# Second input phase: one of the seven block products as seven smaller ones, its operand sums stored and loaded, T3 formed later

## The chip, the cores and the metric

One NeuronCore of a Trainium2 chip runs the kernel. The metric is the time of one execution on the device, in microseconds (us); 911.04 us is the median of three executions of the kernel before (910.7 to 911.11). A profile records one further execution. The engines are TensorE (PE in the profile; PEld is its weight load), VectorE (DVE), ScalarE (ACT), GpSimd (POOL) and SyncE (SP), which only issues transfers.

## What is computed

One layer over 4096 frames of 1024 float32 channels (`DEPTH` is 1, so only the pooling mixer runs):

```python
def pool_mixer(h, in_w, group_w, group_b, scale, out_w):
    b, s, _ = h.shape
    u, gate = jnp.split(h @ in_w, 2, axis=-1)
    ug = u.reshape(b, s, POOL_GROUPS, POOL_GROUP_DIM)
    pooled = jnp.stack([trailing_mean(ug[:, :, g], w) for g, w in enumerate(POOL_WINDOWS)],
                       axis=2) - ug
    mixed = jnp.einsum('bsgc,gcd->bsgd', pooled, group_w) + group_b
    y = mixed.reshape(b, s, POOL_WIDTH) * scale * jax.nn.silu(gate)
    return y @ out_w

h = x + pool_mixer(rms_norm(x, norm_w), ...)
out = rms_norm(h, final_norm_w)
```

The windows are 2, 4, 8 and 16 frames. The large products are `h @ in_w` (1024 by 2048) and `y @ out_w` (1024 by 1024). The kernel has folded `group_w` into the first half of `in_w`.

## The kernel before

**Products.** Every product of a 1024-deep block is done by the Strassen-Winograd scheme: four quarters a11 to a22 of the data and four of the weights b11 to b22, and seven products P1 to P7 of sums of quarters instead of eight. On the data side the sums are S1 to S4, on the weight side T1 to T4. P3 is S4 x b22: S4 = a12 - S2, and b22 unchanged. Each float32 operand is split into a high half (ScalarE's copy, L165 in `split`, L167) and a low half (VectorE's subtraction, L159), both in TensorE's float32r type; a product takes three passes, high x high, high x low, low x high (`mm3`, L598). One product of a block of 1024 frames is 48 matmuls of 128 by 128 by 512 columns.

**Order of the work.** `steps` is one list: phase "a" (channels for windows 2 and 4 with their gate) for four blocks of 1024 frames, phase "b" (windows 8 and 16), which is the second input phase, for four blocks, and phase "o" (the output product) for eight blocks of 512 frames. Each block runs its seven products in the order P1, P2, P7, P6, P5, P4, P3 (`ORDER_IN`) or P1, P7, P6, P2, P5, P4, P3 (`ORDER_OUT`). The main loop (L1325) takes one step per turn: it issues loads up to three steps ahead (`load_reach`), splits the operands of the next step (`advance("split", ...)`), forms sums of the step after that (`form`), issues a pooling that is due (`pool_due`), then the matmuls and the evictions of this step (`run`). A scheduler then puts each engine's instructions in one fixed order, by the order of the program and by what it reckons to be ready; `tc.issue_after` sets an instruction behind another. What comes earlier in the program goes first where both are ready.

**Buffers.** Four operand tiles `op` go round, two for each step, so the split for the next step runs while TensorE works on this one. Eleven tiles `st` and eight tiles `vt` hold everything else (`Slots`); a load waits until its tile is free. Eight PSUM banks: P1, P2, P7, P4 in banks 0 to 3, P6, P5, P3 in banks 4 to 7. After P1 ScalarE copies its banks to banks 4 to 7, where P6, P5 and P3 are added on top.

**Sums of the data.** In phase a `form_in` (L547) forms the sums on VectorE and `split_halves` (L509) stores the operands of P1, P2, P7 and P4 to DRAM (`sd`) through the POOL queue. In phase b these four are loaded (`load_saved`, L528) and the other three, for P6, P5 and P3 (`form_s4`, L592), are formed again by VectorE: six operations on 128 x 1024 per block.

**Eviction and pooling.** P1's chain ends with P3, whose four banks ScalarE copies out (the last branch of `evict_in`, L806). After P5 and P4 VectorE adds the banks onto the rows, and ScalarE applies Silu to the gate. `pool` (L745) then forms the trailing means on VectorE. `pool_later` (L1116) says when: the half from P4 one step after it (two in the last block), the half from P3 two steps after it (five in the last).

**Weights.** Weights of phase b are formed during the last block of phase a (`load_wb`, `form_wb`, `split_wb`). T3, which two of them need, is formed from four stored tiles by `save_t3` (L289) at block 2, P7 of phase a. During block 3 of phase b the weights of the output product are loaded and split behind each step (`load_w`, L343); their sums were formed by `make_wo` (L335) in blocks 1 and 2, at P5.

**The seven inner products of phase o.** From the third block of phase o on, P2 of that phase is itself done by the scheme: `form_inner` (L643), `split_inner` (L669), `product_inner` (L689, matmuls at L701 of 256 columns). Block 1 sets four `st` tiles aside for its weight sums (`kept`).

```python
stages = (P6, P5, P4)
...
    advance("load", n, load, load_reach)
...
    advance("split", n, split_step, split_reach)
...
    pool_due(n)
...
    run(n)
```

Of the kernel before, what the change touches and what calls it, by code (L numbers as in the profile page):

```python
# [15 lines left out]
P = 128  # L16
D = 1024
# [18 lines left out]
class Slots:  # L36
# [4 lines left out]
    def __init__(self, tiles):  # L41
        self.free = deque((0, t) for t in tiles)
        self.used = {}

# [9 lines left out]
    def keep(self):  # L54

        return self.renew(self.free.popleft()[1])

# [7 lines left out]
def kernel(  # L65
# [54 lines left out]

    def renew(t):
        i = next(i for i, u in enumerate(sts) if u is t)
        return mem.tile([P, D], F32R, tag=f"st{i}", name=f"inner{i}")

    st.renew = renew
# [41 lines left out]
    def split(dst, src):  # L167
# [17 lines left out]
        for i in range(P1, P7 + 1)  # L185
# [4 lines left out]
            for i in (P1, P2, P7, P4)  # L190
# [97 lines left out]

    def save_t3():  # L289

        for h in range(2):
            us = []
            for k in (h, 2 + h):
                us.append(take())
                nc.sync.dma_start(out=us[-1], in_=wvd[k])
            with tc.issue_after(evicted[0]):
                sub(us[0], us[1], us[0])
            nc.sync.dma_start(out=t3d[h], in_=us[0])
            for u in us:
                give(u)  # L300
# [22 lines left out]
    def split_wb(i):  # L323
        for h in range(2):
            (u,) = parts.pop((i, h)).values()
            if i == P1:
                split_scaled(w[i][h], u, pair(norm_c, h, 0))
            elif i == P2:
                split_scaled(w[i][h], u, pair(norm_c, h, 1))
            else:  # L330
                split(w[i][h], u)
            if i != P6:
                give(u)
# [202 lines left out]
    def load_in(q, b, i):  # L536
        s = xs[b]
        if i == P1:
            s["11"] = load_saved(b, P1) if q else load_x(b, 0, 0)
        elif i == P2:  # L540
            s["12"] = load_saved(b, P2) if q else load_x(b, 0, 1)
        elif i == P7:
            s["21"] = load_saved(b, P7) if q else load_x(b, 1, 0)
        elif i == P6:
            s["22"] = load_saved(b, P4) if q else load_x(b, 1, 1)

    def form_in(q, b, i):  # L547

        s = xs[b]
        if i in (P1, P2):  # L550
            if q == 0:
                for u in s["11" if i == P1 else "12"]:
                    normalize(b, 0, u)
        elif i == P7:
            if q == 0:
                for h in range(2):
                    normalize(b, 1, s["21"][h])
                    sub(s["21"][h], s["11"][h], s["21"][h])
        elif i == P6:
            s["2"] = [take(pool=early if (q, b) == (0, 0) else None) for _ in range(2)]  # L560
            for h in range(2):
                if q == 0:
                    normalize(b, 1, s["22"][h])
                sub(s["2"][h], s["22"][h], s["21"][h])
            for u in s.pop("21"):
                give(u)
            if q == 0:
                give(rstd.pop(b))
        elif i == P5:
            for h in range(2):  # L570
                add(s["11"][h], s["2"][h], s["11"][h])
            if (q, b) != (0, 0):
                for u in s.pop("2"):
                    give(u)

    def split_in(q, b, i):
        s = xs[b]
        key = {P1: "11", P2: "12", P6: "2", P7: "21", P5: "11", P4: "22", P3: "12"}[i]
        later = q == 0 and b == 0 and i in (P1, P2)
        t = split_halves(s[key], None if q or later else sd[b].get(i))  # L580
        if later:
            stores.extend(zip(sd[0][i], s[key]))
        if i == P6 and (q or b):
            form_s4(b)
        if i not in (P1, P2, P7, P6):
            for u in s.pop(key):
                give(u)
        return t
# [19 lines left out]

    def product_in(i, t, sets, by_bank, between=None, behind=None):
        ps = sets[bank_of[i]]  # L610
# [194 lines left out]

    def evict_in(b, q, i, sets, seeds=4):  # L806
# [22 lines left out]
        elif i == P4:  # L829
            for c, u in enumerate(cells(ev["21"])):  # L830
                add(halved(u), plain(ps[c]), halved(u))
            for u in ev["21"]:
                copy(u, u, AF.Silu)
# [250 lines left out]
    def form(n):  # L1084
        kind, b, i = step(n)
        if kind in ("a", "b"):
            form_in(kind == "b", b, i)
# [16 lines left out]
    def run(n, between=None, behind=None, seeds=4):  # L1104
# [5 lines left out]
        else:  # L1110
            product_in(i, split_up.pop(n), sets, i == P1, between, behind)
            evict_in(b, 0 if kind == "a" else 1, i, sets, seeds)
# [3 lines left out]
    def pool_later(n):  # L1116
        kind, b, i = steps[n]
        if i == P4:
            args = (b, 0 if kind == "a" else 1, 1, ev.pop("22"), ev.pop("21"))
            wait = int(b == 0) if kind == "a" else 1 if b < NB - 1 else 2  # L1120
# [183 lines left out]
    def load_reach(kind, b, i):  # L1304
        return 4 if kind == "o" else 3
# [16 lines left out]
    stages = (P6, P5, P4)  # L1322
    stages = (P6, P5, P4)

    for n in range(2, len(steps)):  # L1325
# [17 lines left out]
        if kind == "o" and b == 1 and len(kept) < 4 and not inner_w:  # L1343
            while len(kept) < 4 and len(st.free) > 2:
                kept.append(st.keep())
            if len(kept) == 4:
                load_inner()
        elif kept:
            keep[0] = 0
        advance("split", n, split_step, split_reach)  # L1350
# [19 lines left out]
        pool_due(n)  # L1370
# [3 lines left out]
        run(n)  # L1374
        if kind == "a" and b == 2 and i == P7:
            save_t3()
# [5 lines left out]
        if kind in ("a", "b"):  # L1382
# [5 lines left out]
            if kind == "b" and b in (1, 2) and i == P5:  # L1388
                make_wo(b - 1)
# [58 lines left out]
```

## Time and profile before

| | |
|---|---|
| median of three executions | 911.04 us (910.7 to 911.11) |
| the profiled execution | 911.84 us |
| its span, first to last instruction | 909.7 us |
| mean granted TensorE clock | 0.997 |
| phase b, from about | 325 to 615 us |
| one block of phase b | 72.6 us |

The profile's page gives busy times per engine, slices of the span, the chain of work that ended last, and groups of equal instructions: line, engine, operation, output <- input, shapes, count, then busy time, mean ns of one, and idle time ahead of them with what ended it. In the timeline a row is start, duration, engine, line, operation, tiles, count, and in brackets the idle time before it. In a table by windows each engine has its busy time and, in brackets, its instructions. A wait row is engine, tile and line, what was waited for, total us, times, longest.

### The profile page before, as it was taken

What the parts mean: (1) busy time and instruction counts of PE and PEld (TensorE: products, weight loads), DVE (VectorE), ACT (ScalarE), POOL (GpSimd) and SP (SyncE); (2) the same over time, 40 slices, a digit from 0 to 9 for tenths busy, and PEclk for the clock granted to TensorE, in tenths of its full rate; (3) what the DMA queues carried; (4) which work ended last, traced back from release to release, by engine and by line L of the source; (5) the groups of instructions that cost most, each with busy time, mean ns of one, the idle gap of its engine ahead of it and who ended that gap; (6) DMA issues with size and microseconds to landing.
All of it is one profiled execution on the core that took longest, in us unless ns stands there. A gap on an engine that the chain in (4) does not pass through costs nothing.

```text
span 909.7 us, 11455 instructions
## 1 busy us (share of the span) xinstructions
PE 900.6 (99%) x4320; PEld 790.1 (87%) x4320; DVE 764.5 (84%) x909; ACT 461.8 (51%) x693; POOL 49.9 (5%) x124
## 2 busy tenths in 40 slices
PE   9999999999999999999999999999999999999997
PEld 7888888888888888888888888888888898888886
DVE  3889995985995997696798699699989878978886
ACT  7869547547446565355445545644424424335334
POOL 0020100100110000000000000000201001001000
PEclk9999999999999999999999999999999999999998
DMA  9977766577675454116616714636385464464332
GB/s 341 401 291 240 276 235 230 189 270 253 217 272 196 156 202 145 47 64 212 255 47 234 275 70 158 235 105 219 137 280 181 149 226 155 146 232 139 116 139 93
DMA packets 66807, 178.08 MB, mean 196 GB/s; under 512 B 6080, under 2 KB 23872, under 8 KB 66752
## 3 DMA queue, kind: packets, MB, share of 16 engines
q1 hardware_dynamic: 60176, 155.83, 48.8%
q0 software_dynamic: 5856, 20.46, 6.1%
q10 hardware_dynamic: 720, 1.06, 0.3%
q8 instruction: 34, 0.56, 0.2%
q14 instruction: 21, 0.17, 0.1%
HBM read 116.50 MB, written 60.83 MB: 195 GB/s over the span
## 4 chain that ended last, share of the span: by engine, by line
PE 91%; DMA 4%; DVE 3%; issue 1%; ACT 0%; SPq 0%; POOL 0%; DVEq 0%; ACTq 0%; POOLq 0%
PE bank L603 88%; PE bank L701 3%; DMA early<-in_wut 2%; DMA st<-in_x 1%; DMA vt<-yd 1%; DVE vt L1033 1%; PE bank L406 1%; DVE op L159 1%; DVE st L159 0%; DVE vt L916 0%; ACT st L943 0%; DVE vt L162 0%; DVE vt L711 0%; SPq L370 0%; DVE st L1033 0%
## 5 line engine op out<-in xcount | busy, mean ns | idle before, releaser
L603 PE MATMUL bank<-op,w 128*128 128x512 f32 x2688 | 580.9, 379 | 0.0
L603 PEld LDWEIGHTS bank<-op,w 128*128 128x128 f32 x2688 | 508.5, 189 | 71.8 <-ACT bank L165 0.4
L603 PE MATMUL bank<-w,op 128*128 128x512 f32 (+1 forms) x1212 | 262.2, 377 | 0.0
L603 PEld LDWEIGHTS bank<-w,op 128*128 128x128 f32 x1212 | 226.3, 189 | 30.7
L165 ACT ACTIVATE op<-st 128x1024 fp32r<-128x1024 f32 x129 | 134.7, 1053 | 142.2 <-PE bank L603 90.5
L159 DVE TENSOR_TENSOR op<-st,op 128x1024 fp32r<-128x1024 f32 x129 | 156.8, 1222 | 51.7 <-ACT op L165 51.3
L156 DVE TENSOR_TENSOR vt<-vt 128x1024 f32<-128x1024 f32 (+6 forms) x72 | 88.2, 1236 | 0.6
L159 DVE TENSOR_TENSOR op<-vt,op 128x1024 fp32r<-128x1024 f32 x43 | 52.5, 1222 | 19.8 <-ACT op L165 19.6
L165 ACT ACTIVATE vt<-bank 128x512 f32<-128x512 f32 x82 | 47.6, 593 | 41.4 <-PE bank L603 40.5
L165 ACT ACTIVATE op<-vt 128x1024 fp32r<-128x1024 f32 x43 | 45.1, 1053 | 39.3 <-PE bank L603 30.2
L159 DVE TENSOR_TENSOR st<-st,st 128x1024 f32<-128x1024 f32 (+1 forms) x43 | 47.0, 1111 | 2.3 <-ACT st L912 1.3
L165 ACT ACTIVATE bank<-bank 128x512 f32<-128x512 f32 x48 | 27.9, 581 | 32.9 <-PE bank L603 32.9
L1033 DVE TENSOR_TENSOR vt<-bank,vt 128x512 f32<-128x512 f32 (+1 forms) x55 | 37.1, 677 | 7.4 <-PE bank L603 7.0
L165 ACT ACTIVATE st<-bank 128x512 f32<-128x512 f32 x48 | 27.8, 593 | 28.7 <-PE bank L603 22.3
L207 POOL TENSOR_SCALAR oms<-oss 128x2 f32<-128x2 f32 x14 | 8.4, 601 | 565.5 <-ACT st L912 460.6
L159 DVE TENSOR_TENSOR w<-st,w 128x1024 fp32r<-128x1024 f32 x25 | 30.2, 1223 | 7.8 <-ACT w L165 7.8
L165 ACT ACTIVATE w<-st 128x1024 fp32r<-128x1024 f32 x25 | 26.0, 1052 | 14.2 <-PE bank L603 9.6
L788 DVE SCALAR_TENSOR_TENSOR st<-vt,colt,st 128x512 f32<-128x512 f32 x46 | 32.7, 752 | 0.1
L1033 DVE TENSOR_TENSOR st<-bank,st 128x512 f32<-128x512 f32 x42 | 28.8, 692 | 3.9 <-PE bank L603 3.7
L783 DVE SCALAR_TENSOR_TENSOR vt<-vt,vt 128x1024 f32<-128x1024 f32 x24 | 29.4, 1227 | 0.3
L916 DVE SCALAR_TENSOR_TENSOR vt<-vt,ors,st 128x1024 f32<-128x1024 f32 x18 | 22.5, 1282 | 7.9 <-POOL ors L225 7.9
L165 ACT ACTIVATE st<-st 128x1024 f32<-128x1024 f32 x16 | 16.9, 1059 | 21.8 <-DVE st L156 21.7
(132 smaller groups left out, 619.0 us busy)
## 6 DMA issues: line engine op xcount, KB each, us to landing
st<-in_x SPq DMA_DIRECT2D x30, 512.0 KB, 5.3
st<-in_xt SPq DMA_DIRECT2D x28, 512.0 KB, 5.6
sd<-st POOLq DMA_DIRECT2D x28, 512.0 KB, 4.6
vt<-in_x SPq DMA_DIRECT2D x27, 512.0 KB, 4.5
st<-sd SPq DMA_DIRECT2D x24, 512.0 KB, 4.2
yd<-st SPq DMA_DIRECT2D x23, 512.0 KB, 2.6
st<-yd SPq DMA_DIRECT2D x20, 512.0 KB, 4.6
out<-vt SPq DMA_DIRECT2D x18, 512.0 KB, 3.6
```

Of the source, the lines that this page charges most:

```text
L156: nc.vector.tensor_tensor(out=dst, in0=a, in1=b, op=ALU.add)
L159: return nc.vector.tensor_tensor(out=dst, in0=a, in1=b, op=ALU.subtract)
L165: return nc.scalar.activation(dst, src, func)
L207: (nc.vector if on_vector and not first else nc.gpsimd).tensor_scalar(out=ms, in0=ss, scalar1=1.0 / D, scalar2=EPS, op0=ALU.mult, op1=ALU.add)
L406: latest[0] = nc.tensor.matmul(ps, a[:, kk, 2 * j + t, :], maps, start=t + m == 0, stop=t == 1 and m == len(pairs) - 1,).ins
L603: latest[0] = nc.tensor.matmul(ps, a, b, start=start and n == 0, stop=stop and n == 2, skip_group_check=True).ins
L701: latest[0] = nc.tensor.matmul(ps, x1, x2, start=i in (P1, P7) and k + n == 0, stop=k == 1 and n == 2, skip_group_check=True,).ins
L783: nc.vector.scalar_tensor_tensor(out=s[:, :, at : at + H], in0=s[:, :, at : at + H], scalar=1.0 / win, in1=v[:, :, HIST:], op0=ALU.mult, o ...
L788: nc.vector.scalar_tensor_tensor(out=sg[:, j], in0=s[:, j, at : at + H], scalar=bias_c[2 * grp + j], in1=sg[:, j], op0=ALU.add, op1=ALU.mult,)
L916: nc.vector.scalar_tensor_tensor(out=us[j], in0=us[j], scalar=rs[:, j : j + 1], in1=fw[0], op0=ALU.mult, op1=ALU.mult,)
L1033: partial["added"] = nc.vector.tensor_tensor(out=dst, in0=src, in1=dst, op=ALU.add).ins
```

## The change

P3 of phase b (S4 times b22) is done by seven inner products in blocks 0, 1 and 2; block 3 keeps the whole product. 48 matmuls of 512 columns become 84 of 256.

- All seven operand sums are stored in phase a and loaded in phase b; `form_in` is only called in phase a. `load_reach` is 2 for most of phase b.
- `form_inner_in` forms and splits the four weight sums of the inner scheme, in block 0 of phase b, into four `st` tiles that are lent (`lend`) until the inner product of block 2 is through (`end`).
- `split_inner_in` forms four data sums of 128 x 512 each; `split_sums` splits them, two by two, in the two `op` tiles of the step that would follow; the split for the following step (`due`) is called inside the product (`then`).
- `inner_in` runs P1, P2, P4, P6, P3, P7, P5. P2, P4 and P3 go on top of the outer chain in banks 4 to 7. P1 goes to bank 0; ScalarE copies it to bank 1, where P6 is added; ScalarE copies that to bank 3, where P5 is added; P7 has bank 2. VectorE adds the four banks onto the rows in six additions.
- In blocks 0 to 2 the Silu of the gate comes after the inner product, and the pooling of the half from P4 two steps after P4 instead of one (in block 3 one instead of two).
- T3: four loads at block 3, P1 of phase a, subtractions and stores one step later. `make_wo` runs at P6 instead of P5. Slots for the inner weights of phase o are set aside from block 0 of that phase on.

```diff
+    def lend(self):
+        t = self.free.popleft()[1]
+        self.lent.append(self.index_of(t))
+        return self.renew(t)
...
-            for i in (P1, P2, P7, P4)
+            for i in ORDER_IN
...
+    def load_t3():
+        for k in range(4):
+            for_t3.append(take())
+            nc.sync.dma_start(out=for_t3[-1], in_=wvd[k])
...
+        if q:
+            t = split_halves(s[i])
+            if i == P3 and inner_at(b):
+                t = split_inner_in(t, s[i])
+            for u in s.pop(i):
+                give(u)
+            return t
...
+    def form_inner_in(stage):
+        pattern, sizes = "p (n k c) -> p n k c", dict(n=2, k=2)
+        if stage == 0:
...
+            sub(t3, b22, b12)
+            add(t2, t3, b11)
+            sub(t1, b22, t2)
+            sub(t4, b21, t2)
...
+        hi, lo = (st.lend().rearrange(pattern, **sizes) for _ in range(2))
+        copy(hi, r)
+        sub(lo, r, hi.bitcast(F32))
...
+    def split_inner_in(ts, us):
+        (a11, a21), (a12, a22) = ([quarter(u, g) for g in range(2)] for u in us)
...
+        sub(s3, a11, a21)
+        sub(s2, a22, s3)
+        sub(s4, a12, s2)
+        add(s1, s2, a11)
...
+    def split_sums(t, n):
+        v, products = t["sums"][n]
+        o = next_op("p (x n k s a) -> p x n k s a", x=2, n=2, k=2, s=2)
+        split(o, v)
...
+    def inner_in(t, sets, then):
+        y, (one, six, seven, five) = sets["y"], sets["v"]
...
+        go(P1)
+        copy(six, one)
+        go(P2)
+        go(P4)
+        go(P6)
+        copied_on = copy(five, six).ins
+        then()
+        go(P3)
+        for c, dst in enumerate(cells(rows, HIST)):
+            with tc.issue_after(copied_on):
+                evicted[0] = copy(halved(dst), plain(y[c])).ins
+        to_rows(one, (0, 0))
+        to_rows(six, (1, 0))
+        go(P7)
+        to_rows(seven, (1, 0), (1, 1))
+        go(P5)
+        to_rows(five, (0, 1), (1, 1))
+        with tc.issue_after(evicted[0]):
+            gates(ev.pop("gates"))
...
-            wait = int(b == 0) if kind == "a" else 1 if b < NB - 1 else 2
+            wait = int(b == 0) if kind == "a" else 2 if inner_at(b) else 1
...
-        advance("split", n, split_step, split_reach)
+        due = lambda: advance("split", n, split_step, split_reach)
+        inside = kind == "b" and i == P3 and inner_at(b)
+        if inside:
+            for half in range(2):
+                split_sums(split_up[n], half)
+        else:
+            due()
+        if kind == "b" and b == 0 and i in in_stages:
+            with tc.issue_after(latest_split[0]), tc.issue_after(latest_copy[0]):
+                form_inner_in(in_stages.index(i))
...
-        pool_due(n)
+        with tc.issue_after(latest_split[0]) if kind == "b" and i == P1 else nullcontext():
+            pool_due(n)
...
-        run(n)
-        if kind == "a" and b == 2 and i == P7:
+        run(n, behind=due if inside else None)
+        if inside and not inner_at(b + 1):
+            st.end()
+        if kind == "a" and b == 3 and i == P1:
+            load_t3()
+        elif for_t3:
             save_t3()
...
-            if kind == "b" and b in (1, 2) and i == P5:
+            if kind == "b" and b in (1, 2) and i == P6:
                 make_wo(b - 1)
```

163 lines of the change are left out of this document (117 added, 46 removed).

## Prediction

> **What bounds the kernel now.** I read the page first (busy shares, then the chain), then the waits of TensorE, then the four blocks of the second input phase.
>
> ```profile
> span 909.7 us, 11455 instructions
> PE 900.6 (99%) x4320; PEld 790.1 (87%) x4320; DVE 764.5 (84%) x909; ACT 461.8 (51%) x693; POOL 49.9 (5%) x124
> PE 91%; DMA 4%; DVE 3%; issue 1%; ACT 0%; SPq 0%; POOL 0%; DVEq 0%; ACTq 0%; POOLq 0%
> PE bank L701 <- DVE vt L711: 0.3, 1, 0.3
> 47.57 655.54 PE bank L603 x3036
> 703.11 3.35 PE bank L701 x30
> ```
>
> The last two rows are the chain in order of time. 3036 matmuls of 512 columns follow each other for 655.54 us without a break: 215.9 ns each, and a step of 48 takes 10.36 us. The 30 of 256 columns take 111.7 ns each. From 47.6 us on TensorE waits once, 0.3 us. So a matmul taken out is time gained, and any wait put in is time lost in full.
>
> ```profile
> core 0: us, PE busy (x) PEld busy (x) DVE busy (x) ACT busy (x) POOL busy (x), PEclk, DMA share, GB/s
> 325.00:397.60 72.60, 72.60 (x338) 63.63 (x337) 59.98 (x65) 34.75 (x48) 0.00 (x0) 1.00 0.33 113
> 470.20:542.80 72.60, 72.60 (x339) 63.63 (x337) 59.48 (x59) 34.37 (x52) 0.00 (x0) 1.00 0.51 182
> 542.80:615.40 72.60, 72.60 (x338) 63.65 (x337) 64.18 (x62) 40.43 (x56) 0.00 (x0) 1.00 0.49 166
> 615.40:651.70 36.30, 36.30 (x170) 31.82 (x169) 36.30 (x41) 10.87 (x15) 0.35 (x1) 1.00 0.54 186
> L159 DVE TENSOR_TENSOR op<-st,op 128x1024 fp32r<-128x1024 f32 x129 | 156.8, 1222 | 51.7 <-ACT op L165 51.3
> ```
>
> These are blocks 0, 2 and 3 of the second input phase and the first 36 us of the output phase, then the group of splits. VectorE is the second engine: 60 of 72.6 us in a block, all of the output phase's start. The split's idle time (51.3 us on ScalarE's half) says that VectorE stands at the instruction in front, with other work behind it. So what counts for VectorE is the order written for it, and where in that order the split stands that TensorE needs next.
>
> **TensorE's part of the change.** Per inner block, 48 matmuls of 512 columns (10.36 us) become 7 x 2 x 2 x 3 = 84 of 256 columns (84 x 111.7 ns = 9.38 us). Three blocks: -2.95, say **-3.0 us**. The rows at 111.7 ns hold both stationary sides in turn, so the exchange of sides should cost nothing.
> The Trainium skill, "TensorE: Matmul & The Clock Gate", section "Back-to-back issue gap", gives columns/2.4 + 2.5 ns, 109 ns here; an estimate by it would be a gain of 3.6 us. The trace has 111.7 ns and decides.
>
> **ScalarE.** Added per inner block: two bank copies and two halves of the sums, about 3 us on an engine that is busy 35 of 72.6 us.
>
> ```profile
> 572.22 1.54 ACT L165 ACTIVATE vt<-bank 128x512 f32<-128x512 f32 x3
> 565.61 2.00 ACT L165 ACTIVATE op<-st 128x1024 fp32r<-128x1024 f32 x2
> ```
>
> A bank copy takes 0.5 us of the engine, a 1024 copy 0.97. Inside the product the chain has room: P1's copy to bank 1 starts after 1.3 us, takes 0.5 and is needed at 4.0 us, where P6 begins; bank 3's starts at 5.4 and is needed at 8.0. Cost 0; if ScalarE were 2 us behind, each late copy would cost its lateness, up to some 1 us a block.
>
> **VectorE, unit prices.** Rows of the hand-over from block 2 to block 3:
>
> ```profile
> 541.57 3.76 DVE L156 TENSOR_TENSOR vt<-vt 128x1036 f32<-128x1036 f32 x3
> 545.24 1.22 DVE L159 TENSOR_TENSOR op<-vt,op 128x1024 fp32r<-128x1024 f32 x1
> 546.38 1.22 DVE L783 SCALAR_TENSOR_TENSOR vt<-vt,vt 128x1024 f32<-128x1024 f32 x1
> 547.51 1.25 DVE L156 TENSOR_TENSOR vt<-vt 128x1052 f32<-128x1052 f32 x1
> 548.68 1.41 DVE L788 SCALAR_TENSOR_TENSOR st<-vt,colt,st 128x512 f32<-128x512 f32 x2
> 550.00 3.79 DVE L156 TENSOR_TENSOR vt<-vt 128x1048 f32<-128x1048 f32 x3
> 567.64 2.36 DVE L159 TENSOR_TENSOR op<-st,op 128x1024 fp32r<-128x1024 f32 x2
> 591.20 0.68 DVE L156 TENSOR_TENSOR vt<-bank,vt 128x512 f32<-128x512 f32 x1
> 591.80 1.22 DVE L159 TENSOR_TENSOR op<-vt,op 128x1024 fp32r<-128x1024 f32 x1
> ```
>
> From start to start: a 1024 split, add or multiply-subtract 1.14 us; a 512 multiply pair 1.32, so 0.66 each; an add out of a bank 0.60; a chain of adds in which each reads the one ahead 1.22 (3.67 for three), 0.1 more each.
>
> Sum of work: gone are six 1024 operations per block (the two differences, two sums, two S4), -6.8 us. Added in an inner block: four 512 sums (2.4), two splits (2.3), six row adds (3.6): +8.3. So VectorE has only 1.5 us more in such a block, and 6.8 less in block 3; block 0 also forms the weight sums, 4 x 0.6 + 2 x 1.14 = 4.7. By amount it would fit. It is the place that decides.
>
> **The pooling moves, and that is the point.** Before, the pooling of the half from P4 was written at P3, that from P3 at P2 of the next block. Now the first is written at P1 of the next block. Each half is 7 adds, 2 multiply-subtracts and 4 short multiplies: 9 x 1.14 + 4 x 0.66 = 12.9 us. In the built order of the changed kernel both halves stand one behind the other in VectorE's queue after the inner product, and the split for P6 of the next block (its tile was free long before, ScalarE's half too) stands behind them. Before, that split was through at 567.64 + 2.36 = 570.0, when TensorE began P6 at about 573.8 (3 steps into block 3).
>
> Let E be the end of an inner product. The last two of the six row adds need its last bank: through at E + 1.3. The next split waits for ScalarE's half, which has the bank copy, four evictions (5 x 0.5), two Silu and itself (3 x 0.97) from E - 3.9 on: E + 1.5. So the queue starts at E + 1.6. P6 begins at E + 3 x 10.36 = E + 31.1; its second matmul needs the split.
> - Block 0 to 1: ahead of and with the split stand 5 splits, 14 adds, 3 multiply-subtracts (22 x 1.14 = 25.1), 6 short ones (4.0), four tiny ones (0.4): E + 31.1 against E + 31.3. Just in time: 0, bounds 0 to 0.6.
> - Block 1 to 2: 23 x 1.14 + 6 x 0.66 = 30.2: E + 31.8, 0.5 late. **+0.5**, bounds 0 to 1.2.
> - Block 2 to 3: here the output weights are split too, and four of these (P1's and P2's) stand ahead: 5 + 4 splits, 14 adds, 4 multiply-subtracts, 27 x 1.14 = 30.8; 8 short ones, 5.3; about 0.5 for adds in a chain. 36.6: E + 38.2. In the built order TensorE does the four matmuls on the high half first and waits at the fifth, E + 31.1 + 0.86 = E + 31.95. **+6.2**, bounds 5.0 (a start 0.6 earlier and 0.6 off the chain) to 7.4.
>
> The next split (op of P6's second half, 1.14 later, needed 4.5 us later) is covered by this wait, and so is P5's.
>
> **The clock after the wait.**
>
> ```profile
> 0.78 3.45 PE L1135 MATMUL bank<-const-bfloat16-1.0 128*128 128x512 bf16 x8 [0.78 <-PEq L1433]
> 900.00:905.00 5.00, 3.01 (x26) 2.79 (x24) 4.35 (x16) 3.85 (x11) 0.00 (x0) 1.00 0.59 227
> 905.00:909.70 4.70, 0.00 (x0) 0.00 (x0) 1.15 (x4) 0.72 (x1) 0.00 (x0) 0.51 0.55 205
> ```
>
> TensorE's last work ends near 903, and from 905 the granted clock is 0.51. At the start eight 512-column matmuls took 3.45 us, 431 ns each, where 216 is the warm rate: 1.7 us lost. No wait of before is long enough to show both in the middle; 6 us of idle time is three times the 2 us after which the clock was down at the end. Bounds: 0 (it doesn't fall) to twice the start's loss, 3.4. I take the start's: **+1.7**.
> The Trainium skill, same page, section "Part 1: The HAM clock gate", says the clock falls to half after an idle window of about 3.4 us and comes back after a busy one. That speaks against this change: an estimate by it is 3.4 to 6.8 us at half rate, 1.7 to 3.4 lost, so that the sum would lie up to 1.7 higher than mine.
>
> **Start of the output phase.** From the split of P5's output weights (TensorE half through P5, E + 46.6; ScalarE's half and its own, done by E + 48.9) to the split for the first block's P6 there stand 24 large operations, 9 bank adds, 4 short ones: 27.4 + 5.4 + 2.6 = 35.4, so E + 84.3; TensorE is there at E + 83.5. 0.8 late, whatever the shift before, since it begins at TensorE. Behind it:
>
> ```profile
> 656.27 2.48 DVE L916 SCALAR_TENSOR_TENSOR st<-st,ors,st 128x1024 f32<-128x1024 f32 x2 [0.92 <-POOL ors L225]
> ```
>
> two such waits of 0.9 us on GpSimd stand between the next splits. **+1.2**, bounds 0 to 3.
>
> **Costed at nothing.** The 24 further loads on SP and 24 further stores on POOL, the four slots lent out, T3 (four loads, two subtractions, two stores, a step or more later than before), and the output weights' sums a step earlier (four loads, eight scalings, four sums, seven stores).
>
> ```profile
> st<-sd SPq DMA_DIRECT2D x24, 512.0 KB, 4.2
> sd<-st POOLq DMA_DIRECT2D x28, 512.0 KB, 4.6
> ```
>
> A load lands 4.2 us after its issue and is asked for two steps (20.7 us) ahead; the cover is 16 us. Behind a store on POOL stand the loads of the next rstd, behind a load on SP the yd stores. POOL is busy 5%, the DMA share of these blocks 0.33 to 0.51. The weights formed from T3 are first used at P7 of block 0 of the second phase, some 70 us after its new place. If the cover goes, a late load costs up to 4.2 us each.
>
> **Sum.** -3.0 + 0 + 0.5 + 6.2 + 1.7 + 1.2 = **+6.6 us**. The profiled execution took 911.84 us (span 909.7 and 2.1 around it): 918.4; the median of before stands 0.8 below it, so **917.6** in a median. All low ends give +2.0 (913.0), all high ones +12.6 (923.6).
>
> **Rivals.**
> - *The splits come in time* (the other side, faster): one mechanism, VectorE's chain after the inner product of block 2. It decides at 30.3 us of work ahead of P6's split; I count 36.6. Below that the wait, the clock's loss and the rest are gone, and -3.0 is left: 908.0. For it: 12 us of VectorE idle per block, and a total that hardly grows. Against: the chain's order is written, and its prices are rows of the same place. 0.09.
> - *Half of it*: a wait near 3 us, too short for the clock, pays back the gain: 911.0, within 0.2%. Needs 3 us off the chain. 0.03.
> - *Transfers*: with 11 - 4 slots a load waits for its slot, or the doubled stores hold a slot in the first phase. Decides when a load is issued less than 4.2 us ahead; three of these add up to 12.6 us: to 930. The built order frees the slots two steps ahead. 0.05.
> - *The change doesn't give what it says*: 256-column matmuls at 123 ns (10.36/84), with the moving side taken from quarters of tiles: no gain, 920.6. Both sides ran at 111.7 before. 0.03.
>
> The forecast has 0.80. The range goes from 913.0 (all low ends) to 922.5 (the last microsecond of the high ends left out); it holds the forecast's case and the fourth rival. About 0.2%, 1.8 us, is what a measurement can tell from no change: faster 0.09, same 0.03, slower 0.88.
>
> **What would show it.** TensorE's waits after: one near 571 us of some 6 us on a split by VectorE, at the fifth matmul of P6 of block 3; next to none at P6 of block 1; a fraction of a microsecond at block 2. Granted clock under 1 in the slice after 571. The 84 matmuls in 9.4 us. VectorE without a break from the inner product of block 2 to that split. The prediction is wrong if VectorE runs the chain in under 31 us, if the split's wait names a DMA, or if TensorE's stretch to 571 is already longer than before.

## The result, and the profile after

The changed kernel takes **925.3 us** (923.6 to 927.62, five runs) where the kernel before takes 911.11 (910.7 to 911.41, five runs): 1.0158 times as long, 95% interval 1.0142 to 1.0175, so 14.2 us slower. Forecast were 917.6, range 913.0 to 922.5: the side was right, the size was not, and the time lies outside the range. The profiled execution of after took 927.62 us, the longest of its five; it is set against the profiled execution of before.

First the page: span, busy time, chain.

```profile
span 924.5 us, 11865 instructions
PE 903.3 (98%) x4428; PEld 793.3 (86%) x4428; DVE 768.0 (83%) x927; ACT 471.9 (51%) x707; POOL 56.2 (6%) x148
PE 73%; DVE 14%; DMA 5%; issue 4%; ACT 2%; POOL 1%; SPq 0%; DVEq 0%; ACTq 0%; POOLq 0%
```

VectorE's total hardly grew (764.5 to 768.0 us), but its share of the chain went from 3% to 14%: its order, not its amount, is what TensorE now waits for. The wait view of TensorE says on what:

```profile
PE bank L631 <- DVE op L177: 11.1, 4, 6.3
PE bank L631 <- ACT vt L183: 1.1, 1, 1.1
PE bank L631 <- ACT st L183: 0.8, 2, 0.5
```

Total, times, longest. Before there was one wait of 0.3 us after the first 47 us; now there are seven, 13.1 us together. The timeline of TensorE places them (start, duration, and in brackets the idle time ahead; the first row is the start of the first phase's products, the rows at 624 and 907 are the first ones of the output phase and the last products; rows without a wait are left out):

```profile
32.70 13.30 PE L631 MATMUL bank<-op,w 128*128 128x512 f32 x60
...
75.93 1.56 PE L631 MATMUL bank<-op,w 128*128 128x512 f32 x6 [0.32 <-ACT st L183]
78.02 309.77 PE L631 MATMUL bank<-op,w 128*128 128x512 f32 x1434 [0.53 <-ACT st L183]
439.81 20.99 PE L631 MATMUL bank<-op,w 128*128 128x512 f32 x96 [1.10 <-ACT vt L183]
502.08 31.13 PE L631 MATMUL bank<-op,w 128*128 128x512 f32 x143 [0.61 <-DVE op L177]
580.86 43.33 PE L631 MATMUL bank<-op,w 128*128 128x512 f32 x188 [6.32 <-DVE op L177]
624.03 10.96 PE L631 MATMUL bank<-w,op 128*128 128x512 f32 x50
635.86 31.35 PE L631 MATMUL bank<-w,op 128*128 128x512 f32 x144 [0.88 <-DVE op L177]
670.50 48.14 PE L631 MATMUL bank<-w,op 128*128 128x512 f32 x214 [3.30 <-DVE op L177]
907.20 10.61 PE L631 MATMUL bank<-w,op 128*128 128x512 f32 x60
```

The same milestones of before:

```profile
33.43 13.30 PE L603 MATMUL bank<-op,w 128*128 128x512 f32 x60
614.89 25.42 PE L603 MATMUL bank<-w,op 128*128 128x512 f32 x117
892.39 10.61 PE L603 MATMUL bank<-w,op 128*128 128x512 f32 x60
```

So the two input phases took 581.5 us and now take 591.3, **+9.9**; the output phase up to its last products took 277.5 and now takes 283.2, **+5.7**; the start came 0.7 earlier. That adds up to the 14.8 us between the spans. Forecast were +5.4 and +1.2.

The granted clock (second last but one column) around the long wait and behind the last one:

```profile
575.00:580.00 5.00, 0.00 (x0) 0.00 (x0) 5.00 (x6) 2.25 (x3) 0.00 (x0) 0.91 1.00 324
580.00:585.00 5.00, 4.14 (x10) 3.30 (x11) 5.00 (x5) 0.00 (x0) 0.00 (x0) 0.50 0.86 306
585.00:590.00 5.00, 5.00 (x23) 4.30 (x22) 1.48 (x2) 0.51 (x1) 0.00 (x0) 0.91 0.95 345
672.00:676.00 4.00, 4.00 (x14) 3.21 (x13) 3.99 (x5) 2.79 (x6) 0.94 (x1) 0.67 0.78 250
```

From 580 to 585 TensorE does 10 matmuls, from 585 to 590 it does 23: it came out of the wait at half clock. VectorE is busy in all of the 10 us to 585. The 188 matmuls behind the wait take 43.2 us from the first of them to the first of the output phase (580.86 to 624.03), where 188 x 215.9 ns are 40.6 (2.6 lost); the 214 behind the wait of 3.30 take 48.0 up to the next row (670.50 to 718.48) for 46.2 (1.8).

### The profile page after: what moved, and what is told of

Read it like the earlier page. It is cut to its first block, busy times and chain, and to the rows that moved or that the text cites. A ratio compares the mean times of both kernels' runs of the same rounds, so it can differ in the third digit from the quotient of the medians.

```text
span 924.5 us, 11865 instructions
## 1 busy us (share of the span) xinstructions
PE 903.3 (98%) x4428; PEld 793.3 (86%) x4428; DVE 768.0 (83%) x927; ACT 471.9 (51%) x707; POOL 56.2 (6%) x148
## 4 chain that ended last, share of the span: by engine, by line
PE 73%; DVE 14%; DMA 5%; issue 4%; ACT 2%; POOL 1%; SPq 0%; DVEq 0%; ACTq 0%; POOLq 0%
PE bank L631 68%; DVE vt L174 7%; PE bank L842 3%; DVE vt L924 2%; DVE op L177 2%; PE bank L715 2%; DVE st L929 1%; DMA early<-in_wut 1%; DMA sd<-st 1%; DMA st<-in_x 1%; PE bank L429 1%; DMA yd<-st 1%; DMA vt<-in_out_w 1%; ACT op L183 1%; DVE vt L929 0%
## 5 line engine op out<-in xcount | busy, mean ns | idle before, releaser
L631 PE MATMUL bank<-op,w 128*128 128x512 f32 x2544 | 554.3, 381 | 8.9 <-DVE op L177 6.9
L631 PEld LDWEIGHTS bank<-op,w 128*128 128x128 f32 x2544 | 481.7, 190 | 79.9 <-DVE op L177 8.0
L177 DVE TENSOR_TENSOR op<-st,op 128x1024 fp32r<-128x1024 f32 x111 | 134.9, 1221 | 47.8 <-ACT op L183 47.3
L183 ACT ACTIVATE op<-st 128x1024 fp32r<-128x1024 f32 x111 | 115.9, 1053 | 88.0 <-PE bank L631 54.1
L183 ACT ACTIVATE op<-vt 128x1024 fp32r<-128x1024 f32 x67 | 70.4, 1055 | 98.9 <-PE bank L631 49.4
L177 DVE TENSOR_TENSOR op<-vt,op 128x1024 fp32r<-128x1024 f32 x67 | 81.3, 1219 | 10.1 <-ACT op L183 10.0
L174 DVE TENSOR_TENSOR vt<-bank,vt 128x512 f32<-128x512 f32 (+1 forms) x59 | 37.8, 679 | 4.1 <-ACT vt L183 2.0
L1180 DVE TENSOR_TENSOR st<-bank,st 128x512 f32<-128x512 f32 x50 | 34.3, 687 | 7.1 <-PE bank L631 6.6
L1180 DVE TENSOR_TENSOR vt<-bank,vt 128x512 f32<-128x512 f32 (+1 forms) x47 | 31.6, 675 | 9.3 <-PE bank L631 9.2
L177 DVE TENSOR_TENSOR st<-st,st 128x1024 f32<-128x1024 f32 (+1 forms) x22 | 24.5, 1124 | 10.5 <-ACT st L264 6.7
L538 POOL DMA_DIRECT2D sd<-st x40 | 21.5, 537 | 126.5 <-DVE st L177 39.3
```

The source lines that it names most:

```text
L174: nc.vector.tensor_tensor(out=dst, in0=a, in1=b, op=ALU.add)
L177: return nc.vector.tensor_tensor(out=dst, in0=a, in1=b, op=ALU.subtract)
L183: return nc.scalar.activation(dst, src, func)
L538: first_saves.append(nc.gpsimd.dma_start(out=saved[h], in_=u).ins)
L631: latest[0] = nc.tensor.matmul(ps, a, b, start=start and n == 0, stop=stop and n == 2, skip_group_check=True).ins
L1180: partial["added"] = nc.vector.tensor_tensor(out=dst, in0=src, in1=dst, op=ALU.add).ins
```

## The experiments

The kernel before ran beside each group, with medians of 911.0 to 911.4. Line numbers are those of the changed kernel, in stores_only those of the kernel before; stores_t3 and warm_wait have their own. Two things have no result. The inner products were not put alone into the kernel before: by my count its second phase holds up to ten of the eleven st tiles, and the inner weights need four. And there is no kernel without inner products in which only the early setting aside of slots is undone: by the code, too few tiles come free in time then.

### The change without its inner products, and with two of three

```diff
     def inner_at(b):
-        return b < NB - 1
+        return False        # loads_only; in inner01: b < NB - 2
...
```

> All of the change but the inner products: the seven sums stored and loaded, T3 and the output weights' sums moved, P3 a whole product in every block, and the half from P4 pooled one step after P4 (in every block, since no block is an inner one). Theory (the written order of VectorE behind an inner product makes TensorE wait at P6 of the next block): no waits at P6 in any block, none at half clock; what is left is the 1.4 us near 76 us behind a store on POOL and the 1.1 us near 439 us behind a load of output weights: about 911.1 + 2.5 = 913.5, between 911 and 915. Rival (the further transfers are the cause): most of the 14.2 us stays, 920 or more. Rival (the 256-column matmuls cost more than the 111.7 ns): no less than 3 us below the changed kernel but no waits gone either.

> The inner products in blocks 0 and 1 only; block 2 does P3 whole and pools its half from P4 a step after P4, as before the change. Theory: the wait of 6.3 us at P6 of block 3 and the 2.5 us at half clock behind it go, 1.0 us of gain goes with the third inner product; VectorE is ahead again at the start of the output phase, so the 0.9 and 3.3 us there and their 1.7 us at half clock go too: 925.3 - 6.3 - 2.5 - 5.9 + 1.0 = 911.6; if the start of the output phase waits all the same, 917.5. The waits near 439 and 502 us stay. Rival (transfers): 921 or more.

loads_only: 916.56 us (ratio 1.0057, 1.0042 to 1.0072). inner01: 916.0 (1.0048, 1.0031 to 1.0064). The wait of 6.3 us and every half-clock stretch are gone in both. So more than a third of the loss, 5.1 us, is there without a single inner product: loads, stores and moves that I had costed at nothing. Two inner products, worth 2.0 us on TensorE, bring 0.6, which the intervals hardly tell from nothing; the third costs 9.3.

### Which of the two halves is in the way

```diff
-            wait = 1 + int(b == 0) if kind == "a" else 2 if b < NB - 1 else 5
+            wait = 1 + int(b == 0) if kind == "a" else 5 if b == NB - 1 else 3 if b == NB - 2 else 2
```

> The changed kernel, but the pooling of block 2's half from P3 is written one step later, so that it stands behind the split for P6 of block 3 in VectorE's queue; the same work, nothing left out. Theory: the wait at the fifth matmul of P6 of block 3 (6.3 us) goes, and the half clock behind it (2.5 us): 925.3 - 8.8 = 916.5, with the waits at 439, 502 and the start of the output phase as they were. VectorE has then less time before the output phase, which can add up to 1.5 us there. Rival (a transfer is late at P6 of block 3): the wait stays at about 6 us.

919.07 us (1.0082, 1.0059 to 1.0105), 6.2 less than the change. The wait of 6.3 us at P6 of block 3 is gone, 0.8 is left at 585. But in its profiled execution, the slowest of four at 921.26 us, the splits are late again at the start of the output phase, ScalarE's by 1.9 and VectorE's by 1.4 us at 628 to 631, with a half clock behind. The mechanism is confirmed; 2.6 of the gain are given back a block later.

```diff
# pool_early: Silu of the gate at P4, P4's half pooled one step later, as before
-            wait = int(b == 0) if kind == "a" else 2 if inner_at(b) else 1
+            wait = int(b == 0) if kind == "a" else 1 if b < NB - 1 else 2
...
```

> The changed kernel (925.3 us), with Silu and the pooling of the half from P4 one step after P4 as in the kernel before, so ahead of the inner product in VectorE's queue (in the last block two steps again). If the two pooled halves that stand behind the inner product are what makes P6's split of block 3 late, the wait of 6.3 us and the half clock after it (2.6) go, and with the place of the last block's half part of the 5 us at the start of the output phase; the row additions now stand behind the pooling, and four banks come free late: 1 to 2 us at blocks 1 to 2 and 2 to 3 by the built order. About 915 to 917. The rival, that VectorE's whole amount of work is too much: the same time is lost at another place, 923 or more.

920.61 us (1.0099, 1.0085 to 1.0113), 4 more than expected. The 6.3 is gone; in its place the row additions of the inner products stand behind the pooling and hold banks: 2.7 us at 474 and 1.3 at 547, 1.3 for a late bank copy at 466, and 3.8 in the output phase. Neither place of this half is free.

### Where the output weights are summed

```diff
-            if kind == "b" and b in (1, 2) and i == P6:
+            if kind == "b" and b in (1, 2) and i == P5:
                 make_wo(b - 1)
```

> The changed kernel with the sums of the output weights formed after P5 again instead of P6, nothing else. Theory: the 1.1 us at P5 of block 1 goes (ScalarE stood at the scaling of weights whose load waited for a tile that the pooling held, with P6's eviction behind it): 924.2, all other waits the same. Rival (that wait is P6's eviction being late by itself): the 1.1 us stays.

927.23 us (1.0169, 1.0146 to 1.0192); the wait at 440 stays (1.2) and one of 1.1 comes at 466. So the earlier place does not make the wait of 1.1. SP's queue points to another cause; first after, then before:

```profile
426.01 0.32 SPq L933 DMA_DIRECT2D yd<-st  x1
428.28 0.38 SPq L249 DMA_DIRECT2D st<-in_out_w  x1
429.42 0.38 SPq L249 DMA_DIRECT2D vt<-in_out_w  x1
```

```profile
415.87 0.32 SPq L792 DMA_DIRECT2D yd<-st  x1
418.53 0.38 SPq L231 DMA_DIRECT2D st<-in_out_w  x1
...
423.65 2.49 SPq L231 DMA_DIRECT2D st<-in_out_w  x3
```

The loads of the output weights (in_out_w) are put on the queue a step earlier in the program, and yet the first is issued 10 us later, behind the store of a pooled half that comes 10 us later too, as the pooling does. The chain ahead of the wait goes through the second load:

```profile
428.16 1.23 DVE vt L924
...
429.42 6.21 DMA vt<-in_out_w
...
435.70 1.32 ACT vt L264 x2
```

It is issued as the pooling's multiply on VectorE gives a vt tile back; behind the load stand ScalarE's scalings, and behind these its eviction, for which TensorE waits. With make_wo at P5 the first load was issued at the same time, 428.2 us; in pool_early, where the pooling comes earlier, the first goes out at 419.1 and the wait at 440 is 0.5. The cause is read from the traces and no run singles it out: in pool3_b2, inner01 and warm_wait, which differ from the change only behind this place, the same wait is 0.5, 0.6 and 0.2, so its size changes from execution to execution.

### The stores of the first phase, and T3

Both kernels, stores_only and stores_t3, start from before. The first stores all seven pairs of sums (nothing reads the three further ones); the second forms T3 where the change forms it, too.

```diff
-            for i in (P1, P2, P7, P4)
+            for i in ORDER_IN
...
-        later = q == 0 and b == 0 and i in (P1, P2)
+        later = q == 0 and b == 0 and i in (P1, P2, P6)
...
```

> The kernel before, with all seven pairs of sums stored in the first phase instead of four (24 more stores); the second phase still forms three of them, and the further stored ones are not read. If the waits of 0.4 and 0.5 us at 76 and 78 us come from the further stores of block 0, which hold tiles that an eviction of the folded weights needs, they are here too, and the time goes from 911.4 to some 912.8. The rival, that they come from some other part of the change (a different order of the block's instructions): no such wait, 911.4.

> The kernel before with all seven pairs of sums stored (917.5 us), and T3 formed where the changed kernel forms it. In that run one wait of 2.8 us stood at 225 us, in the block in which T3's four loads and two stores come between the others, besides 1.0 at 76 to 78. If T3's traffic beside the further stores made that wait, it goes: 914 to 915. The rival, that the further stores alone fill the queue there: the wait stays or moves to another block, 917.5.

stores_only: 917.52 us (1.0063, 1.0051 to 1.0076). stores_t3: 912.11 (1.0008, 0.9999 to 1.0017, eleven runs). The first is 4.7 above what was expected. Its profiled execution, the fastest of its five at 915.03 us, has three waits, and only the first two of them are in after.

```profile
75.99 1.56 PE L603 MATMUL bank<-op,w 128*128 128x512 f32 x6 [0.46 <-ACT st L165]
78.08 144.01 PE L603 MATMUL bank<-op,w 128*128 128x512 f32 x666 [0.53 <-ACT st L165]
224.85 393.95 PE L603 MATMUL bank<-op,w 128*128 128x512 f32 x1824 [2.76 <-ACT st L165]
```

The chain ahead of the third, in order of time, is T3:

```profile
204.10 9.42 DMA st<-wvd
...
213.62 1.24 DVE st L159
...
214.87 3.63 DMA t3d<-st
...
218.56 4.31 DMA st<-wvd
...
222.89 1.24 DVE st L159
```

Beside the further stores a load of T3's takes 9.4 us where 4.1 is the median of these loads before; VectorE's subtraction waits for it, and ScalarE's eviction waits for the subtraction's tile. So moving T3 is worth 5.4 us by the medians (the profiled execution shows 2.8 of it as this wait), all of it the repair of what the stores would break; I had costed it at nothing, and it is nothing only against before. In stores_t3 the two early waits are what is left:

```profile
32.54 13.30 PE L606 MATMUL bank<-op,w 128*128 128x512 f32 x60
615.50 24.77 PE L606 MATMUL bank<-w,op 128*128 128x512 f32 x114
```

These are 582.96 us for the input phases (32.54 to 615.50), 1.50 more than before, with two stops that show 0.95 of idle time. So a stop costs some 0.28 us beyond its idle time.

### The loads alone, and the edits at the output phase one by one

lo_data is before with the data path alone: sums stored and loaded, T3 moved (and, as in the change, the pooling at P1 set behind the latest split). The others start from loads_only (916.6).

```diff
# lo_reach (in load_reach)
-        return 2 if kind == "b" and not early_one else 3
+        return 3
# lo_keep43
-        if kind == "o" and b < 2 and not inner_w and (b or i in (P5, P4, P3)):
+        if kind == "o" and b < 2 and not inner_w and (b or i in (P4, P3)):
```

loads_last2 pools the half from P4 of the last block two steps after it again, lo_kept_last2 also sets the slots aside in block 1 of the output phase, lo_wo has make_wo at P5.

> The kernel before with the changed kernel's data path alone: all seven sums stored, T3 formed later, all sums loaded in the second phase, three steps ahead. The output weights' sums, the pooling and the slots of the output phase stand as in the kernel before. If the loads themselves cost nothing, 912.1 as with the stores and T3 alone, or a little less, since six operations a block are gone from VectorE. The rival, that the loads hold tiles which others need: 914 to 916.6, with waits on evictions into st tiles near 420 to 500 us.

> The kernel without inner products in the second phase (916.6 us), with the half from P4 of the last block pooled two steps after P4 again, as in the kernel before. If the place of this half is what made VectorE late at the start of the output phase (waits of 1.5, 0.7 and 0.9 us at 665, 710 and 714), these go, and the time is 913.5 to 914. The rival, that the slots set aside early make loads of the output phase late: the waits stay, 916.6.

> The kernel without inner products in the second phase (916.6 us), with the setting aside of the four slots for the inner weights of the output phase begun one step later in its first block (at P4, not at P5). If slots that are missing there make VectorE late in the output phase (waits of 1.5, 0.7 and 0.9 us at 665, 710 and 714), a part of these 3 us goes, 914 to 916. The rival, that VectorE's own order there is late and no slot is missing: 916.6, the three waits as they were.

> The kernel without inner products in the second phase (916.6 us), with both edits of the output phase undone together: the slots for the inner weights are set aside in its second block, and the half from P4 of the last block is pooled two steps after P4. If they make the waits at 665, 710 and 714 us (3.0 together), about 913.5. The rival, that the loads two steps ahead and the earlier sums of the output weights make VectorE late: 916 to 917.

> The kernel without inner products in the second phase (916.6 us), with its loads three steps ahead throughout, as in the kernel before. If the shorter lead sets which tiles come free at the start of the output phase, and so the waits at 665 to 714 us (3.0), 913 to 914. The rival, the output weights' sums a step earlier: 916.6.

> The kernel without inner products in the second phase (916.6 us), with the output weights' sums at P5 again. If the earlier place is what costs 3 us, 913 to 914, and the wait of 0.4 at 422 us goes. The rival, the loads two steps ahead: 916.6, waits at 665 to 714 as they were.

| kernel | us | ratio, 95% interval | waits in the output phase |
|---|---|---|---|
| lo_data | 913.02 | 1.0023 (1.0012 to 1.0033) | 0.8 |
| lo_reach | 914.52 | 1.0035 (1.0022 to 1.0047) | 0.3 and 1.6 |
| loads_only | 916.56 | 1.0057 (1.0042 to 1.0072) | 1.5, 0.7, 0.9 |
| lo_keep43 | 916.12 | 1.0054 (1.0042 to 1.0067) | 1.5, 0.4, 0.9 |
| lo_wo | 916.79 | 1.0058 (1.0046 to 1.0071) | 1.5, 0.6, 0.9 |
| loads_last2 | 917.86 | 1.0067 (1.0053 to 1.0081) | 1.4, 1.3, 0.9 |
| lo_kept_last2 | 918.56 | 1.0078 (1.0066 to 1.0090) | 2.2, 0.8 |

The loads themselves cost about 1 us beyond the stores. Of the 3.5 us between lo_data and loads_only the lead of two steps instead of three makes 2.0. The other suspects fell as single causes: the setting aside, a step later, brings 0.4, the place of make_wo nothing, and the last block's pooling, put back, costs 1.3, or 2.0 together with the slots (lo_kept_last2).

### Is the half clock worth its price?

The changed kernel, with 28 matmuls of zeros ahead of P6 of block 3, onto a bank that P6 adds to next.

```diff
+    def fill(bank, count):
+        zeros = zero.broadcast_to([P, H])
+        for _ in range(count):
+            nc.tensor.matmul(bank, warm[:, 0:P], zeros, start=False, stop=False, ...)
```

> The changed kernel (925.3 us) with 28 matmuls of zeros ahead of P6 of block 3, added onto a bank that P6 writes next, so that TensorE is busy for 6.0 of the 6.3 us in which it waited; they change no sum. VectorE's order is the same, so P6 begins at the same time. If the half clock after the wait costs 2.6 us, and idle time alone causes it, the clock stays at 1.0 there and the time is 922.7. The rival, that the clock's fall costs nothing beside the wait because VectorE is late behind it anyway: 925.3, with new waits of 2 to 3 us in the steps behind.

925.87 us (1.0159, 1.0145 to 1.0173): no gain that the intervals can tell, where 2.6 us were hoped for. The clock did stay:

```profile
575.00:581.00 6.00, 5.14 (x24) 2.58 (x23) 6.00 (x7) 1.82 (x3) 0.00 (x0) 1.00 0.95 315
581.00:586.00 5.00, 5.00 (x25) 4.38 (x24) 4.81 (x5) 0.00 (x0) 0.00 (x0) 1.00 0.91 302
```

Behind it stand, one of ScalarE's rows and two of TensorE's:

```profile
588.75 1.06 ACT L183 ACTIVATE w<-st 128x1024 fp32r<-128x1024 f32 x1 [11.93 <-DMA st<-wod]
```

```profile
580.19 10.41 PE L633 MATMUL bank<-op,w 128*128 128x512 f32 x47 [0.86 <-DVE op L177]
591.29 8.90 PE L633 MATMUL bank<-op,w 128*128 128x512 f32 x40 [0.69 <-ACT st L183]
```

Idle time takes the clock, and filling it keeps the clock up. But TensorE, faster now, ran into the next wait: ScalarE had stood 11.9 us before a load of output weights and evicted late. From the end of the wait to the output phase it is 42.3 us (580.19 to 622.47) for 43.2 in after: 0.9 of the 2.6 are won. The new stop takes 1.0 of the rest, and 0.65 goes to three matmuls that came ahead of the wait in after and stand behind the zeros here. 0.3 of what is won go at the output phase's second wait (3.58 for 3.30). The rival was nearer.

### Do the inner products pay when those edits are undone?

Each of these three has three edits undone: slots, last block's pooling, place of make_wo. klw has inner products in three blocks, p3_klw also the moved half of pool3_b2, i01_klw inner products in two.

> The kernel with inner products in blocks 0 and 1 alone (916.0 us), with the slots of the output phase, the last block's pooling and the place of the output weights' sums as in the kernel before. Its waits were 0.96 at 76 to 78, 0.6 at 439, 0.6 at 502 and 3.8 in the output phase. If the output-phase edits make the 3.8, some 912 to 913, the best of the kernels with inner products; to be faster than the kernel before it would have to lose less than 2.0 in all. The rival, that the inner product's work itself makes VectorE late there: 915.5 to 916.5.

> Inner products in three blocks, the half from P3 of block 2 pooled one step later (919.1 us with that edit alone), and the three edits undone as in the run before this one. If the edits of the output phase cost 3 us there too, 916; the rival, that with three inner products VectorE is late from block 2 on by its own amount of work and only the place of the wait changes: 918.5 to 920, waits at 628 to 631 and the half clock as before.

> Inner products in three blocks, with the slots of the output phase, the last block's pooling and the output weights' sums as in the kernel before; block 2's pooling stays where the change puts it. If the wait of 6.3 us comes from that place alone, it is here in full, at the fifth matmul of P6 of block 3, with the half clock behind it, and the time is 915.5 (with one half of the pooling moved) and 6.3 + 0.9 to 2.6 more: 922.5 to 924.5. The rival, that the undone edits shorten VectorE's chain there as well: a wait under 4 us and 918 to 920.

klw: 922.01 us (1.0115, 1.0101 to 1.0129). p3_klw: 915.45 (1.0047, 1.0035 to 1.0059), the best with inner products. i01_klw: 917.39 (1.0071, 1.0059 to 1.0082), with 2.2 at 666 where some 912 to 913 had been hoped for: worse than inner01. First klw, then p3_klw, the rows of block 3's P6:

```profile
581.21 42.73 PE L631 MATMUL bank<-op,w 128*128 128x512 f32 x188 [6.33 <-DVE op L177]
```

```profile
586.10 31.13 PE L631 MATMUL bank<-op,w 128*128 128x512 f32 x143 [0.88 <-DVE op L177]
```

One pooled half a step later takes 6.6 us off: the wait falls from 6.33 to 0.88, and no half clock stands behind it. The wait does not depend on the other edits. These cost the changed kernel 3.3 (klw to after). So the inner products do not pay here: p3_klw takes 2.4 us more than lo_data, which has none (its loads also go three steps ahead), and no version ran faster than the kernel before.

## Why the prediction was right in its mechanism and wrong in its size

**Right.** *TensorE's part*: the chain of after has

```profile
387.79 5.37 PE bank L715 x48
```

so 111.9 ns each, and the gain of 2.95 us holds. *The pooling's place*: waits of none, 0.61 and 6.32 us at P6 of blocks 1, 2 and 3 on VectorE's split, where 0, 0.5 and 6.2 were forecast; pool3_b2, inner01 and the pair klw and p3_klw take it away by the cause named. *ScalarE inside the product* is near its bounds (nothing, or some 1 us where a copy is late): after shows no wait there, klw one of 0.5, i01_klw and pool_early 1.2 and 1.3.

**Wrong, by terms.** Up to the output phase 5.4 were forecast and 9.9 measured; in the output phase 1.2 and 5.7. By the rows of after the first is -2.95, 8.9 of idle time in five stops, 1.4 for their restarts and 2.6 for the clock, 9.9. One of the forecast's own signs of being wrong came true: up to where the fifth matmul of P6 of block 3 is due, TensorE's stretch was 0.8 us longer than before (541.7 for 540.9), not 2.5 shorter.

- *"Costed at nothing"* is the step that failed first: without any inner product the change already costs 5.1 us (loads_only). In the trace of after it shows in the input phases as two terms. The further stores: 0.85 of idle time in two stops, 1.4 with their restarts; by medians 0.8 (stores_t3). The output weights' loads: 1.1, and 1.4 with the restart (none to 1.2 in the other kernels with inner products). The cover that I named (a load asked for 16 us too early) is not what counted. In the first phase it was the store's side: an ACT eviction waits for a tile that a store holds for 9.6 us, while the DMA engines are full,

```profile
65.60 9.57 DMA sd<-st
...
75.28 0.60 ACT st L183
```

  and I had quoted the DMA share of the second phase's blocks, 0.33 to 0.51, not that of the phase that stores: from 60 to 80 us it was 0.79 before,

```profile
60.00:80.00 20.00, 20.00 (x94) 17.55 (x93) 19.97 (x24) 17.04 (x27) 0.96 (x2) 1.00 0.79 292
```

  and is 1.02 after:

```profile
60.00:80.00 20.00, 19.15 (x88) 16.15 (x87) 18.61 (x23) 15.69 (x25) 3.74 (x7) 1.00 1.02 384
```

  The rival "Transfers" named the doubled stores' slots, with a chance of 0.05: it was no rival, but a part that comes on top of the forecast's own case.
- *The clock after the wait*: 1.7 taken, 2.6 by TensorE's rows, 0.9 to 2.6 by its worth, since other work is late behind it too. Its bounds (0 to 3.4) hold it.
- *Restarts*: 0.28 beside each idle time, so some 0.6 for the two waits that were forecast. No term stood for it.
- *"Start of the output phase"*: this is the larger miss, 1.2 for 5.7. Its 0.8 is met (0.88 measured), though not "whatever the shift before": inner01, which is not late at P6 of block 3, has no such wait. What I gave the rest, 0.4 for two waits on GpSimd, was 3.3, and 1.8 at half clock behind it. The step counted VectorE's operations; the wait is for a tile. VectorE's rows:

```profile
654.95 1.42 DVE L929 SCALAR_TENSOR_TENSOR st<-vt,colt,st 128x512 f32<-128x512 f32 x2
...
663.42 1.23 DVE L177 TENSOR_TENSOR st<-st,st 128x1024 f32<-128x1024 f32 x1 [3.69 <-DMA yd<-st]
...
666.83 2.48 DVE L1063 SCALAR_TENSOR_TENSOR st<-st,ors,st 128x1024 f32<-128x1024 f32 x2 [0.92 <-POOL ors L243]
669.23 1.22 DVE L177 TENSOR_TENSOR op<-st,op 128x1024 fp32r<-128x1024 f32 x1
```

  The pooling's last result, through late, is stored to yd, which takes 6.9 us (656.39 to 663.30); the next difference is to be written into the tile that this store holds, and VectorE stands 3.7 us. Then come the norm on GpSimd and the split.

What stays open: which edit hands out just that tile. The waits of the output phase add up to anything from none (stores_only, stores_t3) to 4.7 us (wo_late) in these kernels, and the lead of the loads, the slots and the pooling's place can all shift which of the eleven tiles is the oldest free one; that this is the way they act was not shown. Slots, last block's pooling and make_wo undone together leave 0.7 us near there in klw; taken singly in loads_only (the slots moved by one step) they bring 0.4, lose 1.3 and change nothing. Open too is why single runs of one kernel lie up to 4 us apart (923.6 to 927.62 in after), in pool3_b2 5, where those of before lie 0.7 apart beside it and at most 2.4 in any group; only one execution of each was profiled.

## What to carry to other kernels

Where a change moves work into another engine's queue, count that queue instruction by instruction up to the next hand-over: this was good to 0.1 us here at three hand-overs (0, 0.61 and 6.32 us for 0, 0.5 and 6.2). Where it adds transfers, do not ask only whether the load is early enough: ask who will write next into the tile that the store or the late load holds, and read the DMA share of the stage that gets the transfers. And where one wait is taken away, look at what else was late behind it before counting the gain; the zeros that kept the clock up gained nothing.

## What the runs showed of the hardware

A TensorE at rest for 6.3 us comes back at half clock: the trace records 6.83 us of it (579.1 to 585.9), and 3.41 us that begin just behind the wait of 3.30 (671.3 to 674.7; the wait ends at 670.5). In p3_klw, whose longest stop is 0.88, there is none. The Trainium skill, "TensorE: Matmul & The Clock Gate", section "Part 1: The HAM clock gate", gives an activity window of about 3.4 us. The stretches are one and two such windows long, so the trace agrees.

A stop need not fill such a window to lose the clock. In each of the traces all changes of the clock lie whole multiples of 3.413 us apart (585.93 to 671.26 in after is 25 of them), so the windows can be laid over TensorE's rows. The clock fell behind every window in which TensorE showed 1.93 us of idle time or more, and behind none in which it showed 1.86 or less; only the first 10 us, the start, are left out of this. So the place of a stop counts beside its length: one of 1.94 took the clock in pool3_b2 (all of it in one window, half clock from 628.55 to 635.38), and stops of 2.76 in stores_only and 2.69 in pool_early, each spread over two windows, did not. For the forecast it means that its rival of "a wait near 3 us, too short for the clock" could not count on keeping the clock. Matmuls of zeros in the wait of 6.3 us kept it at 1.00.

Each stop of TensorE cost some 0.28 us more than the idle time that the trace shows (1.50 for 0.95 in two stops of stores_t3), so many short waits cost more than their sum. The starts of the matmuls in after show where it lies: the trace has a matmul end 379 ns after its start where the next one starts after 216, so 0.16 us of every stop are not shown as idle, and the second matmul behind the stops at 75.9, 78.0 and 439.8 starts after 320 ns, 0.10 late.
